# First pairs of the seven-product scheme: fifth and sixth operand first, GpSimd's subtractions last, the fourth a difference of differences

## The chip, the core and the metric

The kernel runs on one core of one Trainium2 chip. A core has a matmul engine (TensorE, PE in the profile; PEld is its loading of weights), VectorE (DVE), ScalarE (ACT), GpSimd (POOL) and SyncE (SP), which issues most of the DMAs here. Each engine works through its own queue in order, and waits on semaphores of the others. PE and the others share the on-chip buffers (SBUF) and the matmul banks (PSUM). The metric is the device time of one execution in microseconds; lower is better.

## What is computed

A decoder trunk of two layers over 1024 positions of width 1024, in float32. Layer 0 mixes tokens with a chunked gating MLP, layer 1 with dilated attention (three groups of dilation 1, 4 and 16); each is followed by a squared-ReLU MLP, and a norm ends it.

```python
def reference(x, mix_norm_g, mlp_norm_g, final_norm_g, a_w_in, ..., w_up, w_down):
    h = x
    for layer in range(DEPTH):
        y = _rms_norm(h, mix_norm_g[layer])
        if layer % N_MIXERS == 0:
            y = _chunk_gating_mixer(y, ...)
        else:
            y = _dilated_attention_mixer(y, ...)
        h = h + y
        y = _rms_norm(h, mlp_norm_g[layer])
        h = h + jnp.square(jax.nn.relu(y @ w_up[layer])) @ w_down[layer]
    return _rms_norm(h, final_norm_g)
```

## The kernel before

**Layout.** Activations are held transposed: `h` is eight tiles of 128 features by 1024 positions. Work goes over two halves of 512 positions (`s` = 0, 1). Every float32 product is made of three passes on rounded operands: a tile is split (`split`, L202) into a high part, copied by ACT (L203), and a low part, subtracted by DVE (L204), and PE runs high·high, high·low, low·high (`three`, L359). So one 128x128 by 128x512 product is three matmuls, and a sum over four feature blocks is twelve.

**Seven products.** The large products (MLP up, MLP down, q/k/v of attention) use a scheme of seven products for a 2x2 block product in place of eight. The two columns are the position halves `s`, the two rows are feature halves `j`. `Terms` (L439) holds the activation operands. With y0, y1 for `s` = 0 and z0, z1 for `s` = 1: operands 1, 2, 3 are y0, y1, z1; t5 = z0 - y0; t6 = z1 - t5; t7 = z1 - z0; t4 = y1 - t6. Each is four tiles (`k` = 0..3), and each tile is split into a `pair` in the pool "s" of 38 slots. `Weights` (L382) loads four raw blocks and forms the seven weight operands, its additions on GpSimd (L401 to L406), its splits on ACT and DVE (tiles "wp", a ring of eight).

**An opening.** Three times the norm of `h` is taken and a stage with seven products starts: MLP 0 (`mlp`, L716), attention (L1474 to L1491) and MLP 1. `first` (L447) scales the eight tiles of `s` = 0 into `kept` and splits them; `second` (L461) does so for `s` = 1 into `raws`, then forms t5 (L476) and t6 (L477) on DVE in the ring "b" of two buffers (`spare`, L131; variables `t1`, `t2`), t7 (L478) and t4 (L479) on GpSimd in place in `kept`, and splits t5 and t6; `rest` (L484) splits t7 and t4. Since z is late, the first pair of weight tiles is done in the classical way (`classical`, L430: eight products, four banks, first all of `s` = 0, then all of `s` = 1); the operands of the seven are made meanwhile. Then PE goes on with products 1, 3, 6, 2, 7, 5, 4 of the next weights.

In an MLP the four banks of a classical half go through Relu (L688) and Square (L689) on ACT, and the result is stored to DRAM (L684) as hidden tiles. Product 1 of the seven is copied out of its bank by ACT at L750 (`first_sum`), and product 2 is then added up in the same bank, so it waits for that copy. In attention the four banks are q, k and v of unit 0 and q of unit 1, evacuated by `out` (L1128): v by ACT (L1079), q and k by ACT (L1121) and DVE (L1122). The next products need banks that these free. Soon after, the first scores, their softmax (DVE L1217, ACT L1219) and the transposes of its result (PE L187) come in.

At the start of attention `h` is stored to DRAM (`hd`, L1489 to L1491) and loaded again later (L1468), which frees eight slots.

**What sets the order.** PE's order is the program's own. `Flow` (L45) keeps a clock of PE's time and runs side tasks (generators such as `second`) when their time has come: a `yield` of so many ns is how long the planner gives a step, and `flow.until` moves the planner's clock on until a condition holds. Only the order comes from this; no engine waits for it. The instructions of the other engines and of the DMA queues are ordered by the framework's scheduler from dependencies, buffers and priority; priority follows the order in the program, and `tc.high_priority(offset=PRIO)` moves instructions ahead. Buffers of a ring are handed out when their last readers are done: "t" has eleven (`temp`), "b" two (`spare`), "r" four (`raw`), PSUM three "mm" and five "at" banks.

Of the kernel before, what the change touches and what calls it, by code (L numbers as in the profile page):

```python
# [10 lines left out]
F32 = mybir.dt.float32  # L11
# [6 lines left out]
P = 128  # L18
D = 1024
S = 1024  # L20
# [92 lines left out]
def trunk(ctx: ExitStack, tc: tile.TileContext, xT, w_u, w_v, w_o, w_s, b_s, w_qkv, w_bo, rel,  # L113
# [17 lines left out]
    def spare():  # L131
        return tpool.tile([P, HALF], F32, tag="b", name="b", bufs=2)
# [22 lines left out]
    def pair(name="y"):  # L155
        return Pair(slot((P, 2, HALF), F32R, name))
# [282 lines left out]
    class Terms:  # L439


        def __init__(self):
            self.blocks = {(j, s): [] for j in range(2) for s in range(2)}
            self.t = {1: self.blocks[0, 0], 2: self.blocks[1, 0], 3: self.blocks[1, 1], 4: [], 5: [], 6: [], 7: []}
            self.kept = []

        def first(self, sq, gi):  # L447

            r = sq.rms()
            yield LAT["rms"]  # L450
            pb = spread(r)
            for k in range(KT):
                if k < 4:
                    self.kept.append(slot((P, 2, HALF), F32, "keep"))
                y = self.kept[k % 4][:, k // 4, :]
                nc.vector.scalar_tensor_tensor(y, h[k][:, sq.cols], vec[:, gi, k:k + 1], pb, op0=ALU.mult, op1=ALU.mult)
                x = pair().split(y)
                yield LAT["tile"]
                self.blocks[k // 4, 0].append(x)

        def second(self, sq, gi):  # L461
            r = sq.rms()
            yield 2 * LAT["rms"]
            pb = spread(r)
            raws = [slot((P, 2, HALF), F32, "raws") for _ in range(4)]
            for j in range(2):
                for k in range(4):
                    o, y = 4 * j + k, raws[k][:, j, :]
                    nc.vector.scalar_tensor_tensor(y, h[o][:, sq.cols], vec[:, gi, o:o + 1], pb, op0=ALU.mult, op1=ALU.mult)
                    x = pair().split(y)  # L470
                    yield LAT["tile"]
                    self.blocks[j, 1].append(x)
            tt = nc.vector.tensor_tensor
            for k, two in enumerate(raws):
                (z0, z1), (y0, y1), t1, t2 = *([t[:, j, :] for j in range(2)] for t in (two, self.kept[k])), spare(), spare()
                tt(t1, z0, y0, op=ALU.subtract)  # L476
                tt(t2, z1, t1, op=ALU.subtract)  # L477
                nc.gpsimd.tensor_tensor(y0, z1, z0, op=ALU.subtract)  # L478
                nc.gpsimd.tensor_tensor(y1, y1, t2, op=ALU.subtract)  # L479
                yield 2 * LAT["tile"]  # L480
                self.t[5].append(pair("t1").split(t1))
                self.t[6].append(pair("t2").split(t2))

        def rest(self):  # L484

            for k, x in enumerate(self.kept):
                t3, t4 = x[:, 0, :], x[:, 1, :]
                if k == 3:
                    t4 = temp()
                    nc.gpsimd.tensor_copy(t4, x[:, 1, :])  # L490
                self.t[7].append(pair("t3").split(t3))
                self.t[4].append(pair("t4").split(t4))

    def start_terms(sq, s, gi, terms):
        flow.add((terms.second if s else terms.first)(sq, gi), (1 + s) * LAT["sum"])


    vg = {}
# [187 lines left out]
    def squared(t, src=None):  # L686

        nc.scalar.activation(t, t if src is None else src, AF.Relu)  # L688
        nc.scalar.activation(t, t, AF.Square)  # L689
# [26 lines left out]
    def mlp(layer, x, first, last):  # L716
# [8 lines left out]
        for s in range(2):  # L725
            banks = [at_bank() if (n < 2) == (s == 1) else mm_bank() for n in range(4)]
            if s == 0:
                banks = [mm_bank() if n < 3 else at_bank() for n in range(4)]
            classical(x, first, s, banks)
            for b, (q, i) in zip(banks, tiles):  # L730
                c[q, i, s] = temp()
                with tc.high_priority(offset=PRIO):
                    squared(c[q, i, s], b)
                what = {(0, 0): 1, (1, 0): 2, (0, 1): (0, 1), (1, 1): 3}[i, s]
                kept(q, {what: c[q, i, s]})
            if s == 0:
                w = up_weights(2)
                for _ in w.steps():
                    pass
# [255 lines left out]
    xa = Terms()  # L995
    firsts = []

    def begin_attention(sq):
        if not firsts:
            firsts.extend(plain(qkv(*t)) for t in (((0, 0), (0, 1)), ((0, 2), (1, 0))))  # L1000
            start_terms(sq, 0, 2, xa)
        else:
            start_terms(sq, 1, 2, xa)

    mlp(0, terms, first, [(half(s), begin_attention) for s in range(2)])

# [468 lines left out]
    for s in range(2):  # L1475
# [3 lines left out]
        classical(xa, firsts, s, banks)  # L1479
        if s == 1:  # L1480
            U[0].bias = bias_tile(U[0].hp, U[0].g)
        for b, tile in zip(banks, ((0, 0), (0, 1), (0, 2), (1, 0))):
            out(tile, s, b)
        if s == 0:
            w = Weights(qkv(*quads[0]), late=FIRST)
            for _ in w.steps():
                pass
    xa.rest()
    hd = [dram.tile([P, S], F32, tag=f"hd{k}", name=f"hd{k}", bufs=1) for k in range(KT)]  # L1489
    for k in range(KT):  # L1490
        nc.sync.dma_start(hd[k], h[k])  # L1491

    for n, two in enumerate(quads):
        wn = Weights(qkv(*quads[n + 1])) if n + 1 < len(quads) else None
# [123 lines left out]
```

## Time and profile before

| | us |
| --- | --- |
| median of 3 runs | 2185.85 |
| lowest to highest | 2181.33 to 2186.66 |
| profiled execution, its time | 2182.13 |
| span of the profile, first to last instruction | 2180.4 |
| PE busy | 2121.8 (97%) |
| DVE busy | 1647.1 (76%) |
| ACT busy | 1126.3 (52%) |
| GpSimd busy | 600.9 (28%) |

A row of the timeline has the start and the length in us, the engine, the line of the code, the operation, the tiles written and read (buffer numbers left out), the shape, and the count of instructions merged in it. In brackets stands the engine's idle time before it, and which instruction's end released it. In a row of the waits stand the waiting engine and line, then the engine, tile and line waited for, the total, the number and the longest. A row for one line of the code has the least, median and greatest duration in ns, and the first and last start in us. A row of the stretches has the stretch, its length, then for PE, PEld, DVE, ACT and POOL the busy time with the number of instructions, the granted PE clock, and DMA. A matmul's end is modelled, so the time of a run of matmuls is taken from start to start. "y" are split tiles of `kept` and `raws`; "t" as a matmul's operand is a split t4, t5, t6 or t7.

### The profile page before, as it was taken

The numbers are of one execution on the slowest core, as the hardware profiler recorded it, in microseconds if no ns is written. First come the engines' busy times: TensorE is split into PE (matmuls) and PEld (weight loads), VectorE is DVE, ScalarE is ACT, GpSimd is POOL, SyncE is SP. The second block draws the span as 40 slices with busy tenths as digits, with TensorE's granted clock in tenths as the row PEclk, the third lists the DMA queues.
The fourth block names the chain that finished last, engine by engine and source line by source line (L and its number), as shares of the span: only waits on it lengthen the run. The fifth ranks groups of instructions, "written<-read, shape, count | busy, mean of one in ns | idle before, by whom it ended". The sixth has DMA issues, their size and how long they took to land.

```text
span 2180.4 us, 30158 instructions
## 1 busy us (share of the span) xinstructions
PE 2121.8 (97%) x10242; PEld 1755.2 (80%) x10242; DVE 1647.1 (76%) x2987; ACT 1126.3 (52%) x2266; POOL 600.9 (28%) x442
## 2 busy tenths in 40 slices
PE   7999999999999999998999999999999999999998
PEld 5888887888878888886888788887878888788887
DVE  5875349676689888878787877878786666988886
ACT  5743225555564444346665656665455555544443
POOL 1100115333223322533212222201343232333345
PEclk9999999999999999999999999999999999999999
DMA  6221213456354444321211111141055543644432
GB/s 222 87 88 45 62 41 96 158 189 198 138 176 160 159 141 137 105 82 39 52 46 46 43 48 45 46 147 62 20 169 193 184 159 113 203 150 146 157 104 78
DMA packets 158814, 247.04 MB, mean 113 GB/s; under 512 B 33481, under 2 KB 47940, under 8 KB 158660
## 3 DMA queue, kind: packets, MB, share of 16 engines
q1 hardware_dynamic: 157760, 243.89, 34.3%
q8 instruction: 80, 1.31, 0.2%
q10 hardware_dynamic: 900, 1.23, 0.2%
q14 instruction: 74, 0.61, 0.1%
HBM read 180.41 MB, written 64.66 MB: 112 GB/s over the span
## 4 chain that ended last, share of the span: by engine, by line
PE 82%; DVE 9%; ACT 3%; issue 2%; DMA 2%; POOL 0%; SPq 0%; DVEq 0%; ACTq 0%; POOLq 0%
PE at L180 41%; PE mm L180 39%; PE at L187 2%; DVE wp L204 2%; DVE t L204 1%; ACT t L1219 1%; ACT wp L203 1%; DVE k L1122 1%; DMA t<-hid 1%; DVE tr L204 0%; DMA r<-in_w_v 0%; DVE h L332 0%; DVE q L1122 0%; DVE h L893 0%; DMA h<-hd 0%
## 5 line engine op out<-in xcount | busy, mean ns | idle before, releaser
L203 ACT ACTIVATE wp<-r 128x512 fp32r<-128x512 f32 (+3 forms) x492 | 295.1, 605 | 458.0 <-PE at L180 287.7
L180 PE MATMUL mm<-y,wp 128*128 128x512 f32 x1608 | 405.2, 398 | 12.8 <-ACT t L750 6.6
L180 PE MATMUL at<-hx,wp 128*128 128x512 f32 x1770 | 413.8, 390 | 3.8 <-DVE wp L204 2.2
L204 DVE TENSOR_TENSOR wp<-r,wp 128x512 fp32r<-128x512 f32 (+3 forms) x492 | 380.9, 778 | 40.1 <-ACT wp L203 36.3
L180 PEld LDWEIGHTS at<-hx,wp 128*128 128x128 f32 x1770 | 331.8, 188 | 75.1 <-DVE h L893 3.3
L180 PEld LDWEIGHTS mm<-y,wp 128*128 128x128 f32 x1608 | 303.2, 191 | 80.4 <-ACT t L750 7.5
L180 PE MATMUL at<-t,wp 128*128 128x512 f32 x1344 | 314.3, 389 | 0.0
L180 PEld LDWEIGHTS at<-t,wp 128*128 128x128 f32 x1344 | 252.7, 188 | 52.7 <-DVE t L756 0.2
L401 POOL TENSOR_TENSOR t<-r 128x512 f32<-128x512 f32 (+3 forms) x78 | 112.8, 1446 | 624.8 <-DMA r<-in_w_dn 270.3
L403 POOL TENSOR_TENSOR r<-r 128x512 f32<-128x512 f32 (+3 forms) x78 | 118.4, 1518 | 326.9 <-DVE wp L204 320.1
L180 PE MATMUL mm<-t,wp 128*128 128x512 f32 x768 | 192.6, 398 | 0.0
L204 DVE TENSOR_TENSOR hx<-t,hx 128x512 fp32r<-128x512 f32 x192 | 179.8, 948 | 5.7 <-ACT hx L203 5.6
L261 POOL TENSOR_TENSOR t<-t 128x512 f32<-128x512 f32 (+1 forms) x54 | 69.1, 1280 | 387.3 <-ACT t L252 385.4
L180 PE MATMUL mm<-hx,wp 128*128 128x512 f32 x708 | 171.8, 389 | 0.0
L180 PEld LDWEIGHTS mm<-t,wp 128*128 128x128 f32 x768 | 141.2, 189 | 29.8
L180 PE MATMUL mm<-y,whi 128*128 128x512 f32 x512 | 158.1, 390 | 0.0
L180 PEld LDWEIGHTS mm<-hx,wp 128*128 128x128 f32 x708 | 132.8, 188 | 28.1 <-DVE b L919 0.6
L893 DVE TENSOR_TENSOR h<-h,at 128x512 f32<-128x512 f32 x144 | 97.5, 679 | 55.4 <-PE at L180 55.3
L180 PE MATMUL at<-y,wp 128*128 128x512 f32 x552 | 138.1, 391 | 0.0
L756 DVE TENSOR_TENSOR t<-t,at 128x512 f32<-128x512 f32 x116 | 79.0, 683 | 74.9 <-PE at L180 74.7
L203 ACT ACTIVATE hx<-t 128x512 fp32r<-128x512 f32 x192 | 118.4, 628 | 27.8 <-DMA t<-hid 23.4
L406 POOL TENSOR_TENSOR r<-r 128x512 f32<-128x512 f32 (+3 forms) x78 | 107.2, 1374 | 79.8 <-issue 54.0
(213 smaller groups left out, 3244.0 us busy)
## 6 DMA issues: line engine op xcount, KB each, us to landing
t<-hid SPq DMA_DIRECT2D x194, 256.0 KB, 5.0
hid<-t SPq DMA_DIRECT2D x140, 256.0 KB, 2.7
r<-in_w_up SPq DMA_DIRECT2D x128, 256.0 KB, 2.8
r<-in_w_dn SPq DMA_DIRECT2D x88, 256.0 KB, 2.7
r<-in_w_qkv SPq DMA_DIRECT2D x72, 256.0 KB, 2.6
hid<-b SPq DMA_DIRECT2D x56, 256.0 KB, 2.7
r<-in_w_v SPq DMA_DIRECT2D x48, 256.0 KB, 3.0
h<-in_xT SPq DMA_DIRECT2D x16, 256.0 KB, 4.5
```

Of the source, the lines that this page charges most:

```text
L180: nc.tensor.matmul(out, lhsT, rhs, **kw)
L187: nc.tensor.transpose(out, src, ident)
L203: nc.scalar.activation(hi, src, AF.Copy)
L204: nc.vector.tensor_tensor(lo, src, hi.bitcast(F32), op=ALU.subtract)
L261: nc.gpsimd.tensor_tensor(self.acc, self.acc, sq, op=ALU.add)
L401: tt(r3, r[0, 0], r[1, 0], op=ALU.subtract)
L403: tt(r[1, 1], r[1, 0], r[0, 0], op=ALU.subtract)
L406: tt(r[0, 0], r[0, 1], r[1, 1], op=ALU.subtract)
L756: nc.vector.tensor_tensor(out, x, y, op=ALU.add)
L893: engine.tensor_tensor(hs[i, s], hs[i, s], src, op=ALU.add)
L1122: nc.vector.scalar_tensor_tensor(lo, a, sc, hi.bitcast(F32), op0=ALU.mult, op1=ALU.subtract)
L1219: nc.scalar.activation(p[:, c], p[:, c], AF.Exp, bias=m, scale=-1.0, accum_out=dn)
```

## The change

In `Terms`: `first` also subtracts, on GpSimd and in place, y0 from y1 once y1 is split; t5 and t6 are formed in tiles of the general ring "t" of eleven, for each `k` one step ahead of their splits, and the planner is given 1600 ns a step; after all of them GpSimd forms t7 = z1 - z0 and t4 = (y1 - y0) - t7, and sets `formed`, for which `rest` waits in the planner. A callable `then` runs once the rows of `s` = 1 are scaled: in attention it stores `h` to DRAM, which stood after `xa.rest()`. In `mlp` only the Relus out of the banks keep the high priority; the four Squares and the stores follow them. In attention the classical outputs of `s` = 1 are evacuated in the order 2, 3, 0, 1. PE's instructions are the same in number; GpSimd has four more subtractions an opening.

```diff
-            self.kept = []
+            self.kept, self.formed = [], False
...
                 self.blocks[k // 4, 0].append(x)
-
-        def second(self, sq, gi):
+                if k >= 4:
+                    nc.gpsimd.tensor_tensor(y, y, self.kept[k % 4][:, 0, :], op=ALU.subtract)
+
+        def second(self, sq, gi, then=None):
...
-            tt = nc.vector.tensor_tensor
-            for k, two in enumerate(raws):
-                (z0, z1), (y0, y1), t1, t2 = *([t[:, j, :] for j in range(2)] for t in (two, self.kept[k])), spare(), spare()
-                tt(t1, z0, y0, op=ALU.subtract)
-                tt(t2, z1, t1, op=ALU.subtract)
-                nc.gpsimd.tensor_tensor(y0, z1, z0, op=ALU.subtract)
-                nc.gpsimd.tensor_tensor(y1, y1, t2, op=ALU.subtract)
-                yield 2 * LAT["tile"]
-                self.t[5].append(pair("t1").split(t1))
-                self.t[6].append(pair("t2").split(t2))
+            if then:
+                then()
+            tt, sums = nc.vector.tensor_tensor, []
+            for k in range(5):
+                if k < 4:
+                    z, y0, t1, t2 = raws[k], self.kept[k][:, 0, :], temp(), temp()
+                    tt(t1, z[:, 0, :], y0, op=ALU.subtract)
+                    tt(t2, z[:, 1, :], t1, op=ALU.subtract)
+                    sums.append((t1, t2))
+                if k:
+                    for p, t in zip((5, 6), sums[k - 1]):
+                        self.t[p].append(pair(f"t{p}").split(t))
+                yield LAT["tile"]
+            for z, y in zip(raws, self.kept):
+                nc.gpsimd.tensor_tensor(y[:, 0, :], z[:, 1, :], z[:, 0, :], op=ALU.subtract)
+                nc.gpsimd.tensor_tensor(y[:, 1, :], y[:, 1, :], y[:, 0, :], op=ALU.subtract)
+            self.formed = True

         def rest(self):

+            flow.until(lambda: self.formed)
...
                 with tc.high_priority(offset=PRIO):
-                    squared(c[q, i, s], b)
+                    nc.scalar.activation(c[q, i, s], b, AF.Relu)
+            for q, i in tiles:
+                nc.scalar.activation(c[q, i, s], c[q, i, s], AF.Square)
...
+    hd = [dram.tile([P, S], F32, tag=f"hd{k}", name=f"hd{k}", bufs=1) for k in range(KT)]
+
+    def spill():
+        for k in range(KT):
+            nc.sync.dma_start(hd[k], h[k])
...
-            start_terms(sq, 1, 2, xa)
+            start_terms(sq, 1, 2, xa, spill)
...
-        for b, tile in zip(banks, ((0, 0), (0, 1), (0, 2), (1, 0))):
+        outs_ = list(zip(banks, ((0, 0), (0, 1), (0, 2), (1, 0))))
+        for b, tile in outs_[2:] + outs_[:2] if s else outs_:
             out(tile, s, b)
...
     xa.rest()
-    hd = [dram.tile([P, S], F32, tag=f"hd{k}", name=f"hd{k}", bufs=1) for k in range(KT)]
-    for k in range(KT):
-        nc.sync.dma_start(hd[k], h[k])
```

More of the change, by code (lines that the diff above doesn't have):

```diff
@@ L492, in rest, with start_terms @@
                 self.t[4].append(pair("t4").split(t4))
-    def start_terms(sq, s, gi, terms):
-        flow.add((terms.second if s else terms.first)(sq, gi), (1 + s) * LAT["sum"])
+    def start_terms(sq, s, gi, terms, *then):
+        flow.add((terms.second if s else terms.first)(sq, gi, *then), (1 + s) * LAT["sum"])
     vg = {}
```

## The prediction

> **What bounds the kernel now.** I read the page first, then PE's waits, then PE's rows where those waits lie, and last the queues of ACT, DVE and GpSimd at the same moments. From the page:
>
> ```profile
> PE 2121.8 (97%) x10242; PEld 1755.2 (80%) x10242; DVE 1647.1 (76%) x2987; ACT 1126.3 (52%) x2266; POOL 600.9 (28%) x442
> ```
>
> PE is the bound, so an edit is worth what it takes out of PE's idle time and its slowed matmuls. Two of PE's longest waits name tiles beside the change (us, times, longest); in the stretch with the second, PE is busy 4.35 us of 10 at a granted clock of 0.77:
>
> ```profile
> PE mm L180 <- ACT t L750: 6.6, 2, 4.3
> PE mm L180 <- ACT t L1079: 5.6, 1, 5.6
> ```
>
> ```profile
> 990.00:1000.00 10.00, 4.35 (x14) 3.24 (x13) 9.90 (x11) 7.84 (x13) 5.16 (x4) 0.77 0.10 25
> ```
>
> They are the three openings, where a stage turns from classical products to the seven: MLP 0 near 367, attention near 992, MLP 1 near 1589. Each is sized from PE's rows, first MLP 0:
>
> ```profile
> 365.67 1.29 PE L180 MATMUL at<-t,wp 128*128 128x512 f32 x5
> 369.31 4.22 PE L180 MATMUL mm<-y,wp 128*128 128x512 f32 x12 [2.35 <-ACT t L750]
> 373.34 11.59 PE L180 MATMUL at<-t,wp 128*128 128x512 f32 x48
> 384.76 2.88 PE L180 MATMUL mm<-y,wp 128*128 128x512 f32 x12
> 387.48 5.60 PE L180 MATMUL at<-t,wp 128*128 128x512 f32 x24
> ```
>
> Undisturbed, 12 matmuls take 2.72 us from start to start (384.76 to 387.48), 0.227 each. The five of the first row are over at 366.80; the 60 up to 384.76 should take 13.60 and take 17.96. The opening loses **4.36**: the gap, and 2.0 of slow matmuls behind it. MLP 1, then attention:
>
> ```profile
> 1585.81 2.88 PE L180 MATMUL at<-t,wp 128*128 128x512 f32 x12
> ...
> 1592.97 4.51 PE L180 MATMUL mm<-y,wp 128*128 128x512 f32 x12 [4.28 <-ACT t L750]
> 1597.32 7.87 PE L180 MATMUL at<-t,wp 128*128 128x512 f32 x34
> ```
>
> ```profile
> 987.47 4.24 PE L180 MATMUL mm<-y,wp 128*128 128x512 f32 x18
> 997.35 4.21 PE L180 MATMUL mm<-y,wp 128*128 128x512 f32 x9 [5.65 <-ACT t L1079]
> 1001.49 1.32 PE L180 MATMUL at<-k,q 64*128 64x128 f32 x12
> ...
> 1009.63 0.33 PE L187 MATMUL at<-ident,t 128*128 128x128 f32 x1 [1.30 <-ACT t L1219]
> ```
>
> MLP 1: the 12 matmuls from 1585.81 end at 1588.53. The next 12 should end 2.72 later; they end 8.79 later, at 1597.32, so **6.07** is lost. Attention: the 18 matmuls (six classical ones and the first of the seven products) end at 991.55; the next start at 997.35, and nine take 4.14 where 2.04 would do: 5.80 + 2.10 = **7.90** lost by 1001.49. A second wait, of the transposes for the first softmax, follows at 1009.63.
>
> ACT works in order, and what PE wants from it (L750, L1079) stands behind splits that come late. MLP 0, then attention:
>
> ```profile
> 358.63 0.63 ACT L203 ACTIVATE t<-b 128x512 fp32r<-128x512 f32 x1 [2.02 <-DVE b L477]
> 359.17 3.22 ACT L203 ACTIVATE t<-keep 128x512 fp32r<-128x512 f32 x6
> ...
> 368.65 0.61 ACT L750 ACTIVATE t<-mm 128x512 f32<-128x512 f32 x1
> ```
>
> ```profile
> 991.98 0.63 ACT L203 ACTIVATE t<-b 128x512 fp32r<-128x512 f32 x1 [3.37 <-DVE b L476]
> ...
> 996.25 1.05 ACT L1079 ACTIVATE t<-mm 128x512 f32<-128x512 f32 x1
> ```
>
> The "b" ring has two buffers. The next pair of t1, t2 waits until GpSimd has read t2 (L479) and both splits are done; and while GpSimd runs, a subtraction on DVE takes about 1.7 instead of 0.69 (two in 3.48, one in 0.69):
>
> ```profile
> 342.58 0.69 DVE L477 TENSOR_TENSOR b<-raws,b 128x512 f32<-128x512 f32 x1
> 343.19 3.48 DVE L204 TENSOR_TENSOR t<-b,t 128x512 fp32r<-128x512 f32 x2
> ...
> 365.93 0.67 DVE L204 TENSOR_TENSOR wp<-r,wp 128x512 fp32r<-128x512 f32 x1
> ```
>
> ```profile
> L478 POOL TENSOR_TENSOR keep<-raws x12: 1292/1710/1846, 331.3 to 1579.2; 128x512 f32<-128x512 f32 x12
> ```
>
> **Fifth and sixth first, in general buffers.** The number and size of DVE's and ACT's instructions stay as they are. What goes is the ring's turn-round: GpSimd no longer stands between one k and the next. In MLP 0 the last "b" split ran at 358.63, and 9.48 us of ACT's work (the "keep" splits, weight splits, four Relus, four Squares) lay between 359.17 and L750. At 342.58 the second k had its t2, and GpSimd had two of its eight subtractions behind it. With all t1, t2 at hand it needs for the other six and the two weight steps L403 and L406 eight times 1.74 (half of 3.48, the pace at which DVE and GpSimd take turns), 13.9: until 356.5, an estimate from these rows. PE's classical products end three products of 12 before 366.80, at 358.64, so the "keep" splits are through by then. ACT owes PE four Relus and L750, five times 0.54 (3.22 / 6), 2.7, and has until 366.80. The gap goes, and the slow matmuls with it. Next late is weight 2: its low part, done at 366.60 (365.93 + 0.67), is wanted by the product's third matmul at 367.25, so it holds even if DVE gains nothing. 4.36 at best, 0 if ACT's order stays; I take **4.2**, since the wait of 2.02 at 358.63 is what filled that queue.
>
> In MLP 1 the same split is the bound that is left:
>
> ```profile
> 1589.13 0.68 DVE L204 TENSOR_TENSOR wp<-r,wp 128x512 fp32r<-128x512 f32 x1
> ```
>
> It ends at 1589.81 and is wanted at 1588.53 + 0.45 = 1588.98: between 0 and 0.83 late, as DVE does or doesn't gain. Of 6.07 I take **5.7**.
>
> **Attention.** Here DVE is the tight engine:
>
> ```profile
> 957.25 0.75 DVE L469 SCALAR_TENSOR_TENSOR raws<-h,vec,at 128x512 f32<-128x512 f32 x1 [3.48 <-PE at L187]
> ...
> 971.60 0.71 DVE L477 TENSOR_TENSOR b<-raws,b 128x512 f32<-128x512 f32 x1
> 975.40 0.69 DVE L1070 TENSOR_TENSOR V<-at,V 128x512 fp32r<-128x512 f32 x1 [3.09 <-ACT V L1069]
> ...
> 1002.13 4.69 DVE L204 TENSOR_TENSOR t<-keep,t 128x512 fp32r<-128x512 f32 x6
> ...
> 1008.77 0.27 DVE L1217 CUSTOM_DVE_ANT_0 t<-at,b 128x128 f32<-128x128 f32 x1
> ```
>
> The 5.65 at L1079 goes, as ACT's splits no longer wait; evacuating the mm banks first brings L1079 ahead of two other tiles. But then PE comes 7.9 earlier to the transposes of 1009.63, which need the softmax of 1008.77, and DVE has nearly all of its work still to do. So this term is what DVE gains before 1008.77: at least the 3.09 that it stood idle at 975.40, which the freed subtractions fill; at most PE's 7.9, if L1217 also passes the six "keep" splits of 1002.13 (4.69). How DVE's queue will be ordered this trace can't show; the present one puts the splits first, so I stay near the low end: **4.5**. Below 3.09 it comes only if GpSimd's turns fill that idle time.
>
> **GpSimd.** The fourth operand as a difference of differences costs four more subtractions an opening, in the first half's pass: 4 x 1.71 = 6.8 of GpSimd, and on DVE up to 4 x 1.05 (1.74 less 0.69). In attention they end in the 3.48 that DVE idles ahead of 957.25, waiting for PE's turn: 0, and at worst 4.2 - 3.48 = 0.7 for what that cover doesn't hold. Eight subtractions stay in the second half, now without a claim on t2; nothing on PE waits for them before products 7 and 4, the fifth and last of the seven in this first pair.
>
> **Buffers and the planner.** Eight sums go through the ring "t" of eleven, which also takes the evacuated banks. No row shows a wait for it; the nearest is the 2.02 at the "b" ring, so 0 to 2 an opening. I take 0: a sum is free after its split, without GpSimd. The new wait for "formed" is the planner's, not an engine's: five steps of 1600 in place of four of 3200 let it pass earlier than before, so PE's order stays. 0.
>
> **Relu apart from Square, order of evacuation.** Four Squares (2.2 at 0.54) lose their priority and can go behind L750; the stores of hidden tiles on SP's queue wait for them, and the next weights' loads behind those. The 48 matmuls from 373.34 carry no wait, so these loads come in time now; I take 0, bounds minus 2.2 to plus 2.2. In attention the mm banks are emptied first, so L1079 passes two tiles of the at banks; that is part of the 7.9.
>
> **h to DRAM.** The stores run early already:
>
> ```profile
> 932.36 12.58 SPq L1491 DMA_DIRECT2D hd<-h  x8
> ```
>
> They are issued by 944.94, before the second half's rows are scaled (from 957.25), so moving the statement up brings them no earlier: 0. Should the queue put them behind the scaling (over by 971.60), they would hold SP until 984.2, still ahead of the end of classical at 988.83: 0 again.
>
> Sum: 4.2 + 5.7 + 4.5 = 14.4. The profiled execution took 2182.13 (span 2180.4), so 2167.7; the median of 2185.85 lies 3.7 above it, and in its terms the forecast is **2171.4**.
>
> The trace has the 2.35 gap followed by 12 matmuls in 4.03 (369.31 to 373.34), not 2.72. The Trainium skill (TensorE: Matmul & The Clock Gate, "What's actually happening") has the clock halved only after an idle window of about 3.4 us; by that, the gap in MLP 0 would cost its 2.35 alone and the sum would be 2.35 + 5.7 + 4.5 = 12.6, not 14.4. The row decides: a gap below that length did slow the matmuls here.
>
> **Rivals** (times in the median's terms).
> - *DVE is the bound in attention all along.* The stall only moves from 997 to the transposes, which start at 1009.6 as before. For it: DVE's 9.90 of 10 busy in 990 to 1000. Against: the 3.09 idle. Gain 4.2 + 5.7 = 9.9: 2176.0.
> - *The change doesn't unblock ACT.* The splits' order on ACT stays ahead of L750 and L1079. Then only the Squares (2.2) leave the queue in each MLP, and about 1 (one evacuation, L1079's 1.05) comes from the other order in attention: gain 5.4, 2180.5. For it: the order is the scheduler's, not the code's. Against: the ring's waits are in the rows.
> - *GpSimd's tail holds ACT (slower).* If its eight subtractions start only after the last t2, the "keep" splits on ACT wait for them, with L1079 behind. In attention the seven sums left at 971.60 end, by 1.74 each, at 983.8; eight subtractions and the weights' two reach 1001.2; with a copy (1.71 at most), two splits (1.1) and L1079 (1.05) it is 1005.1, and PE resumes 7.8 later than at 997.35. With the MLPs as before that is 2193.6; if each still gains the Squares' 2.2, 2189.3. It turns slower from where the last subtraction ends after about 993.5 (997.35 less those 3.9). Against: GpSimd's first subtraction ran at 331.3, 11 us before the second k's t2, so its queue isn't kept for last.
>
> **Chances.** The forecast has 0.62, the first rival 0.15, the second 0.13, the third 0.10. The forecast's own gain runs from 9 to 20: below, the Squares' 2.2 and a ring wait against it; above, all of 4.36 + 6.07 + 7.90 and the 1.30 at 1009.63, 19.6. That is 2166 to 2177; with the scatter of the runs shown (2181.33 to 2186.66, half of it 2.7) below and the second rival above, the range is 2163 to 2181. A measurement of this kernel can tell about 0.3%, 6.6 us, from no change. Faster by more: the forecast and the first rival, 0.77. Within it: the second and half of the third, 0.18. Slower: the other half, 0.05.
>
> **What would show it.** Right: no PE wait on L750 in either MLP and the 12 matmuls behind it in 2.72; L1079 before 991.6; the "t" splits no longer waiting on DVE's "b"; a PE wait for L1219 as the largest left in attention. Wrong: "keep" splits on ACT waiting for GpSimd; PE waiting for weight 2 or the seventh operand; loads of the next weights late behind the hidden stores.

## The result, and the profile after

| | before | after |
| --- | --- | --- |
| median, us (17 runs each) | 2185.10 | 2187.91 |
| lowest to highest | 2180.01 to 2188.96 | 2185.54 to 2192.01 |
| span of the profiled execution | 2180.4 | 2184.8 |

The ratio is 1.0015, 95% interval 1.0008 to 1.0021. By the bound of 0.3% this is no change, with a sign: a little slower. The forecast was 2171.4, range 2163 to 2181.

The page of the kernel after has the engines' busy times, and its waits of PE have the lines that replace those of before (L750 is now L762, L1079 is L1097, L756 is L768, L476 and L477 are L481 and L482, L478 and L479 are L489 and L490):

```profile
PE 2120.8 (97%) x10242; PEld 1752.7 (80%) x10242; DVE 1660.3 (76%) x2987; ACT 1126.3 (52%) x2266; POOL 617.3 (28%) x454
```

```profile
PE mm L180 <- ACT t L1097: 9.1, 1, 9.1
...
PE mm L180 <- ACT t L762: 6.0, 2, 5.2
...
PE mm L180 <- DVE h L332: 2.5, 4, 1.3
...
PE at L180 <- DVE t L768: 2.2, 1, 2.2
```

DVE does the same 2987 instructions in 13.2 us more; GpSimd, with twelve more, is busy 16.4 us longer. The two waits that were to go are there: the one in attention has grown from 5.6 to 9.1, that in MLP 0 from 2.4 to 5.2; only MLP 1's shrank, to 0.8. PE's timeline after, in MLP 0, attention and MLP 1:

```profile
364.12 2.88 PE L180 MATMUL at<-t,wp 128*128 128x512 f32 x12
372.18 4.95 PE L180 MATMUL mm<-y,wp 128*128 128x512 f32 x12 [5.18 <-ACT t L762]
376.96 9.28 PE L180 MATMUL at<-t,wp 128*128 128x512 f32 x40
...
991.32 4.24 PE L180 MATMUL mm<-y,wp 128*128 128x512 f32 x18
1004.68 3.77 PE L180 MATMUL mm<-y,wp 128*128 128x512 f32 x9 [9.12 <-ACT t L1097]
1008.38 0.95 PE L180 MATMUL at<-k,q 64*128 64x128 f32 x12
...
1594.89 3.06 PE L180 MATMUL mm<-y,wp 128*128 128x512 f32 x12 [0.84 <-ACT t L762]
1597.78 5.60 PE L180 MATMUL at<-t,wp 128*128 128x512 f32 x24
1605.54 5.76 PE L180 MATMUL at<-t,wp 128*128 128x512 f32 x24 [2.16 <-DVE t L768]
```

By the prediction's count (0.227 a matmul, start to start), attention has lost 13.36 - 4.08 = 9.28 at the gap and 3.70 - 2.04 = 1.66 in the nine slow matmuls: 10.94, where it was 7.90.

For a sum over everything I took, for each matmul in the trace, the distance to the next one's start less the median distance for its shape and line, and added this up for the 100 us around each opening. "PE's loss" below is this number.

| PE's loss, us | MLP 0 (300 to 400) | attention (950 to 1050) | MLP 1 (1550 to 1650) | all else |
| --- | --- | --- | --- | --- |
| before | 5.0 | 17.6 | 5.9 | 55.2 |
| after | 9.7 | 20.2 | 4.0 | 54.3 |

The four differences (+4.7, +2.6, -1.9, -0.9) make 4.5; the span grew by 4.4. So, in these two profiles, the whole result is made in the three openings. (The medians lie 2.8 apart. Some 1.6 us of such a difference in one opening can be the phase of the clock; see the last section.)

What is late there is seen on DVE. The views of one line of code give the least, median and greatest duration of the sums t5 and t6; before:

```profile
L476 DVE TENSOR_TENSOR b<-raws,keep x12: 673/686/1780, 325.4 to 1577.4; 128x512 f32<-128x512 f32 x12
...
L477 DVE TENSOR_TENSOR b<-raws,b x12: 675/692/1820, 335.8 to 1581.6; 128x512 f32<-128x512 f32 x12
```

After:

```profile
L481 DVE TENSOR_TENSOR t<-raws,keep x12: 670/1776/1784, 340.5 to 1577.2; 128x512 f32<-128x512 f32 x12
...
L482 DVE TENSOR_TENSOR t<-raws,t x12: 677/1668/1779, 341.2 to 1578.4; 128x512 f32<-128x512 f32 x12
```

The median sum went from 0.69 to 1.7 us, at the same number and size. GpSimd's timeline in attention shows what runs beside them: in after its eight subtractions stand in one unbroken row, at the same time as DVE's sums.

```profile
976.20 1.80 POOL L489 TENSOR_TENSOR keep<-raws 128x512 f32<-128x512 f32 x1 [12.78 <-DVE t L481]
978.08 1.63 POOL L490 TENSOR_TENSOR keep<-keep 128x512 f32<-128x512 f32 x1
...
988.30 1.62 POOL L490 TENSOR_TENSOR keep<-keep 128x512 f32<-128x512 f32 x1
991.15 1.67 POOL L403 TENSOR_TENSOR r<-r 128x512 f32<-128x512 f32 x1 [1.23 <-DVE wp L204]
992.90 1.62 POOL L406 TENSOR_TENSOR r<-r 128x512 f32<-128x512 f32 x1
```

In before the ring of two parted these subtractions, and the weight sums L403 and L406 ran between them, from 978.02 to 981.34:

```profile
978.02 1.62 POOL L403 TENSOR_TENSOR r<-r 128x512 f32<-128x512 f32 x1 [4.29 <-issue]
979.72 1.62 POOL L406 TENSOR_TENSOR r<-r 128x512 f32<-128x512 f32 x1
```

In after they end at 994.52. ACT, in order, waits for them, with the evacuation behind:

```profile
994.55 1.15 ACT L203 ACTIVATE wp<-r 128x512 fp32r<-128x512 f32 x2 [10.17 <-POOL r L406]
...
996.65 3.73 ACT L203 ACTIVATE t<-keep 128x512 fp32r<-128x512 f32 x7
...
1000.81 1.04 ACT L1139 ACTIVATE q<-at 128x512 fp32r<-128x512 f32 x1
...
1002.70 1.04 ACT L1139 ACTIVATE k<-at 128x512 fp32r<-128x512 f32 x1
1003.54 1.09 ACT L1097 ACTIVATE t<-mm 128x512 f32<-128x512 f32 x1
```

### The profile page after: what moved, and what is told of

It is laid out like the page before. It is cut to its first block, busy times and chain, and to the rows that moved or that the text cites. A ratio compares the mean times of both kernels' runs of the same rounds, so it can differ in the third digit from the quotient of the medians.

```text
span 2184.8 us, 30158 instructions
## 1 busy us (share of the span) xinstructions
PE 2120.8 (97%) x10242; PEld 1752.7 (80%) x10242; DVE 1660.3 (76%) x2987; ACT 1126.3 (52%) x2266; POOL 617.3 (28%) x454
## 3 DMA queue, kind: packets, MB, share of 16 engines
q10 hardware_dynamic: 900, 1.23, 0.2%
## 4 chain that ended last, share of the span: by engine, by line
PE 81%; DVE 10%; ACT 3%; DMA 3%; issue 2%; SPq 1%; POOL 0%; DVEq 0%; ACTq 0%; POOLq 0%
PE at L180 40%; PE mm L180 39%; PE at L187 2%; DVE wp L204 2%; DVE t L204 1%; DMA t<-hid 1%; DVE t L481 1%; DVE t L482 1%; DVE y L204 1%; SPq L169 1%; ACT wp L203 1%; DVE k L1140 1%; ACT t L1237 0%; DMA r<-in_w_up 0%; DVE q L1140 0%
## 5 line engine op out<-in xcount | busy, mean ns | idle before, releaser
L204 DVE TENSOR_TENSOR wp<-r,wp 128x512 fp32r<-128x512 f32 (+3 forms) x492 | 388.3, 793 | 39.5 <-ACT wp L203 36.0
L403 POOL TENSOR_TENSOR r<-r 128x512 f32<-128x512 f32 (+3 forms) x78 | 116.4, 1493 | 318.9 <-DVE wp L204 316.9
L768 DVE TENSOR_TENSOR t<-t,at 128x512 f32<-128x512 f32 x116 | 79.0, 683 | 76.2 <-PE at L180 76.0
L406 POOL TENSOR_TENSOR r<-r 128x512 f32<-128x512 f32 (+3 forms) x78 | 106.8, 1370 | 82.5 <-issue 53.8
```

The costliest lines, as they stand in the source:

```text
L204: nc.vector.tensor_tensor(lo, src, hi.bitcast(F32), op=ALU.subtract)
L403: tt(r[1, 1], r[1, 0], r[0, 0], op=ALU.subtract)
L406: tt(r[0, 0], r[0, 1], r[1, 1], op=ALU.subtract)
L768: nc.vector.tensor_tensor(out, x, y, op=ALU.add)
```

## The experiments

**Theory 1, the burst:** without the ring GpSimd runs its eight subtractions in one row beside DVE's sums and splits; the two engines slow each other, and weight sums, weight splits and the evacuations behind them on ACT come late. **Theory 2, ACT's order:** the evacuation order and the Squares, or the sums' stay in the ring "t", are what hold L762 and L1097. Ratios are to the kernel before on the same chip.

**x1_tail_dve:** the kernel after, the second half's eight subtractions on DVE.

```diff
-                nc.gpsimd.tensor_tensor(y[:, 0, :], z[:, 1, :], z[:, 0, :], op=ALU.subtract)
-                nc.gpsimd.tensor_tensor(y[:, 1, :], y[:, 1, :], y[:, 0, :], op=ALU.subtract)
+                nc.vector.tensor_tensor(y[:, 0, :], z[:, 1, :], z[:, 0, :], op=ALU.subtract)
+                nc.vector.tensor_tensor(y[:, 1, :], y[:, 1, :], y[:, 0, :], op=ALU.subtract)
```

> The changed kernel with the eight subtractions of the second half (t7, t4) on DVE in place of GpSimd. Theory 1 (burst): freed from the ring, GpSimd runs its eight subtractions in one row beside DVE's eight sums, each sum takes 1.7 instead of 0.69, and behind them come the weights' low splits, GpSimd's L403 and L406 and so ACT's queue. Then here the sums take 0.7, the wait for L1097 falls from 9.1 to under 4, that for L762 in MLP 0 from 5.2 to under 2.4, and the time is some 8 us under the changed kernel, about 2180. Theory 2 (order and buffers: ACT's order, the late Squares or the ring t): DVE has 8 x 0.69 = 5.5 us more to do an opening and nothing is freed, so the waits stay or grow: 2188 to 2193.

2170.98 us, ratio 0.9943 (0.9929 to 0.9956). Giving DVE eight more instructions an opening saves some 16 us against after (1.0015 less 0.9943, of 2185). One of these subtractions takes 0.68 on DVE, and the sums are back at 0.68:

```profile
L482 DVE TENSOR_TENSOR t<-raws,t x12: 678/684/693, 340.8 to 1559.3; 128x512 f32<-128x512 f32 x12
...
L489 DVE TENSOR_TENSOR keep<-raws x12: 677/682/686, 354.7 to 1570.5; 128x512 f32<-128x512 f32 x12
```

PE's wait on L762 is gone, L1097's is 5.1, and MLP 1 loses 0.0. Theory 1 holds, though its sizes were off: the gain is twice what it expected, and the wait on L1097 was to fall under 4.

**x2_first_dve:** the kernel after, the first half's four subtractions (L461) on DVE.

```diff
-                    nc.gpsimd.tensor_tensor(y, y, self.kept[k % 4][:, 0, :], op=ALU.subtract)
+                    nc.vector.tensor_tensor(y, y, self.kept[k % 4][:, 0, :], op=ALU.subtract)
```

> The changed kernel with the four new subtractions of the first half (y1 - y0) on DVE in place of GpSimd. Theory 1: the new wait of 1.34 for h (L332) in MLP 0 goes, as no split of y is slowed in front of that addition; the waits for L762 and L1097 stay. 1 to 3 us under the changed kernel: 2185 to 2187. Theory 2: nothing of this counts, 2188; DVE's own 4 x 0.69 could make it 1 to 2 slower.

2191.73 us, ratio 1.0039 (1.0024 to 1.0054): a miss. In MLP 0's first half DVE is itself what PE waits for, the additions to `h` (L332); four more instructions ahead of them made that wait longer, not shorter. PE's timeline of x2:

```profile
313.08 0.94 PE L180 MATMUL mm<-y,wp 128*128 128x512 f32 x3 [2.93 <-DVE h L332]
...
314.63 3.73 PE L180 MATMUL mm<-y,wp 128*128 128x512 f32 x9
```

In after the same wait was 1.34. The waits of the second half (L762 5.2, L1097 9.1) were the same as in after.

**x3_evac_only:** the kernel before, with Relu and Square apart and the order of output, and nothing else.

```diff
-                    squared(c[q, i, s], b)
+                    nc.scalar.activation(c[q, i, s], b, AF.Relu)
+            for q, i in tiles:
+                nc.scalar.activation(c[q, i, s], c[q, i, s], AF.Square)
...
-        for b, tile in zip(banks, ((0, 0), (0, 1), (0, 2), (1, 0))):
+        outs_ = list(zip(banks, ((0, 0), (0, 1), (0, 2), (1, 0))))
+        for b, tile in outs_[2:] + outs_[:2] if s else outs_:
```

> The kernel before with only the Relus apart from the Squares and the other order of evacuation; operands as before. Theory 1: these edits are harmless, 0 to 3 us under the kernel before (2182 to 2185): L750 comes up to 2.2 earlier, L1079 about 1. Theory 2: they are what costs, so the waits are as long as in the changed kernel and the time is 2187 to 2189.

2181.13 us, ratio 0.9987 (0.9976 to 0.9997). Harmless, perhaps a small gain. Of PE's waits, that on the first sum's copy, here L752, falls from 6.6 to 4.3 and a wait for DVE comes instead; attention's is untouched.

```profile
PE mm L180 <- ACT t L1081: 5.6, 1, 5.6
PE mm L180 <- ACT t L752: 4.3, 2, 3.0
...
PE at L180 <- DVE t L758: 1.9, 1, 1.9
```

**x4_no_tail:** the kernel after without the eight subtractions; products 7 and 4 run on other data, so its time is that of less work.

```diff
-                nc.gpsimd.tensor_tensor(y[:, 0, :], z[:, 1, :], z[:, 0, :], op=ALU.subtract)
-                nc.gpsimd.tensor_tensor(y[:, 1, :], y[:, 1, :], y[:, 0, :], op=ALU.subtract)
+                pass
```

> The changed kernel without the eight subtractions of the second half: t7 and t4 are taken from what stands in their buffers, so the products 7 and 4 work on other data, in the same shapes. Theory 1: no contention is left in the second half and the whole of the waits for L762 and L1097 goes: 10 to 16 us under the changed kernel, 2172 to 2178. Theory 2: ACT's order and the ring stay, so at most 3 us under it, 2185.

2168.41 us, ratio 0.9932 (0.9918 to 0.9946), below the range of theory 1. L762's wait is gone, L1097's is 1.4. So GpSimd's eight subtractions cost some 18 us (1.0015 less 0.9932), and doing them on DVE, about 2 of that (x1; the two intervals overlap). Theory 2 falls with x1, x3 and x4: the order edits cost nothing, and with them in place the time comes down.

The next two separate the ring from the engine.

**y1_before_dve:** the kernel before, its L478 and L479 on DVE; the ring of two stays.

```diff
-                nc.gpsimd.tensor_tensor(y0, z1, z0, op=ALU.subtract)
-                nc.gpsimd.tensor_tensor(y1, y1, t2, op=ALU.subtract)
+                nc.vector.tensor_tensor(y0, z1, z0, op=ALU.subtract)
+                nc.vector.tensor_tensor(y1, y1, t2, op=ALU.subtract)
```

> The kernel before, with its eight second-half subtractions an opening (L478, L479) on DVE instead of GpSimd; the ring of two for t1, t2 stays. Burst theory: what costs is GpSimd subtracting beside DVE, in before too, so without it the sums on DVE take about 0.69 each and the time is 2171 to 2176, close to the run with the tail on DVE (2171.0), ring or no ring. Ring theory (the prediction's reading: the turn-round of the ring is what held ACT): GpSimd is out of the turn, but both splits of a k still stand between it and the next, so only part of the gain comes: 2177 to 2182.

2173.91 us, ratio 0.9959 (0.9946 to 0.9971), as the burst theory had it.

**y3_ring_only:** the kernel before, t5 and t6 in the ring of eleven.

```diff
-                (z0, z1), (y0, y1), t1, t2 = *([t[:, j, :] for j in range(2)] for t in (two, self.kept[k])), spare(), spare()
+                (z0, z1), (y0, y1), t1, t2 = *([t[:, j, :] for j in range(2)] for t in (two, self.kept[k])), temp(), temp()
```

> The kernel before with t1 and t2 in the general ring of eleven in place of the ring of two, and nothing else: GpSimd's two subtractions still stand behind each k's sums in the program. Burst theory: with the ring gone GpSimd and DVE meet as in the kernel after, whatever the statements' order: 2182 to 2188, the waits on L1079 and L750 not less than in before. Rival (the ring is what held ACT, and the kernel after loses by putting GpSimd's subtractions last and adding four): 2172 to 2178, with the wait on L1079 under 3.

2186.49 us, ratio 1.0011 (1.0003 to 1.0020). One word makes what the whole change made; its waits of PE in attention and the MLPs are

```profile
PE mm L180 <- ACT t L1079: 9.1, 1, 9.1
PE mm L180 <- ACT t L750: 7.7, 2, 5.1
```

and its t5 sums took 1.78 in the median:

```profile
L476 DVE TENSOR_TENSOR t<-raws,keep x12: 670/1779/1785, 338.8 to 1576.1; 128x512 f32<-128x512 f32 x12
```

| ratio to before | subtractions on GpSimd | on DVE |
| --- | --- | --- |
| ring of two | 1 (before) | 0.9959 (y1) |
| ring of eleven | 1.0011 (y3), 1.0015 (after) | 0.9943 (x1) |

The ring moves the time by 0.11 to 0.16%, some 3 us, up with the subtractions on GpSimd and perhaps down with them on DVE (there the two intervals overlap); the engine moves it by 0.4 to 0.7%, 9 to 16 us. (x1 has the change's other edits too.)

Nor did the ring of two keep the engines apart. Take DVE's 128x512 TENSOR_TENSOR instructions of the second halves (325 to 400, 935 to 1010, 1530 to 1610) and add up what each took above 0.69: 44.8 us in before, 49.0 in y3, 47.6 in after, but 21.5 in y1 and 18.3 in x1. With or without the ring DVE loses about the same to GpSimd; without it more of the loss falls on the sums, which the splits wait for.

Two runs ask how the burst costs.

**z3_wsum_dve:** the kernel after with L403 and L406 of each opening's first weights on DVE, so that they don't stand behind the burst.

```diff
             r, tt = self.r, nc.gpsimd.tensor_tensor
+            t2 = nc.vector.tensor_tensor if self.late == FIRST else tt
...
-            tt(r[1, 1], r[1, 0], r[0, 0], op=ALU.subtract)
+            t2(r[1, 1], r[1, 0], r[0, 0], op=ALU.subtract)
...
-            tt(r[0, 0], r[0, 1], r[1, 1], op=ALU.subtract)
+            t2(r[0, 0], r[0, 1], r[1, 1], op=ALU.subtract)
```

> The kernel after, GpSimd's burst as it is, with the two last weight sums (L403, L406) of the first seven-product weights of each opening on DVE, so that no weight stands behind the eight subtractions on GpSimd's queue. If the burst costs by its length on GpSimd (weights late, and ACT's splits of them holding L762 and L1097): most of the gain of the runs without the burst comes, 2172 to 2178, and L1097's wait falls under 5. If it costs by slowing DVE's sums and splits from 0.69 to 1.7: DVE has two more such subtractions, 2184 to 2190, the waits as in after.

2183.40 us, ratio 0.9996 (0.9984 to 1.0007): under the second range and far above the first, some 4 us below after. The queue behind the burst is a part of the cost. The larger part stays, and ACT's wait in attention only became shorter (10.17 to 6.19); it now ends with DVE:

```profile
993.57 1.15 ACT L203 ACTIVATE wp<-r 128x512 fp32r<-128x512 f32 x2 [6.19 <-DVE r L407]
```

**z4_held:** the kernel after with GpSimd's eight held until the last t6 is formed.

```diff
+            for y in self.kept:
+                nc.gpsimd.tensor_copy(y[:, 0, 0:1], sums[3][1][:, 0:1])
             for z, y in zip(raws, self.kept):
```

> The kernel after with GpSimd's eight subtractions held until the last t6 is formed: four copies of one column of it (128x1) are put ahead of them, into columns that they overwrite, so the result is the same. The weights' two sums then come before the burst, and DVE's eight sums run without GpSimd beside them. Burst theory by DVE's slowed sums: the sums take about 0.69 again, the t splits come early, 2176 to 2183. Rival 3 of the prediction (GpSimd's tail itself holds ACT's splits of keep, with L1097 behind): the wait on L1097 stays at 9 or more, 2187 to 2193.

2189.19 us, ratio 1.0021 (1.0011 to 1.0031). The sums took 0.68 again, as expected, and yet nothing was gained: the burst now ran beside the splits, and L406 ended at 998.05.

```profile
L481 DVE TENSOR_TENSOR t<-raws,keep x12: 669/684/1776, 342.8 to 1576.8; 128x512 f32<-128x512 f32 x12
```

```profile
998.08 1.15 ACT L203 ACTIVATE wp<-r 128x512 fp32r<-128x512 f32 x2 [12.50 <-POOL r L406]
```

So it isn't the sums as such. In both places tried, the burst lengthens DVE's and GpSimd's work together, and ACT waits for the last of it. Of my own theory the narrow form (only the slowed sums) fell here. What stands is that both queues count; no run separates their shares further, since in attention the hold also put L403 and L406 behind most of the burst.

The rest looks for the best place of these operands on DVE.

**y2_all_dve:** t4 = y1 - t6 on DVE right behind t6, t7 at the tail on DVE, nothing in the first half.

```diff
-                if k >= 4:
-                    nc.gpsimd.tensor_tensor(y, y, self.kept[k % 4][:, 0, :], op=ALU.subtract)
...
                     tt(t2, z[:, 1, :], t1, op=ALU.subtract)
+                    tt(self.kept[k][:, 1, :], self.kept[k][:, 1, :], t2, op=ALU.subtract)
...
-                nc.gpsimd.tensor_tensor(y[:, 0, :], z[:, 1, :], z[:, 0, :], op=ALU.subtract)
-                nc.gpsimd.tensor_tensor(y[:, 1, :], y[:, 1, :], y[:, 0, :], op=ALU.subtract)
+                nc.vector.tensor_tensor(y[:, 0, :], z[:, 1, :], z[:, 0, :], op=ALU.subtract)
```

> The kernel after with no subtraction of the openings on GpSimd: none in the first half, t4 = y1 - t6 on DVE right behind t6, and t7 = z1 - z0 on DVE at the tail. Against the run with only the tail on DVE (2171.0) it saves the 1.34 wait on h in MLP 0 (and what the first half loses in the others) and does four additions fewer an opening, all on DVE: eight instead of twelve. Burst theory: 2165 to 2170. If the first half's subtractions on GpSimd are free: 2170 to 2172. If DVE's own load is now the bound, t4 ahead of the splits of t5 and t6 costs as much as it saves: 2171 to 2174.

2174.88 us, ratio 0.9956 (0.9944 to 0.9968): the third case, just above its range. MLP 0 loses 4.9, by a wait of 2.3 on DVE's L766 and slow matmuls behind it.

**z1_tail_two:** the same with t4 = y1 - t6 at the tail.

```diff
-                    tt(self.kept[k][:, 1, :], self.kept[k][:, 1, :], t2, op=ALU.subtract)
...
-            for z, y in zip(raws, self.kept):
+            for z, y, (_, t2) in zip(raws, self.kept, sums):
                 nc.vector.tensor_tensor(y[:, 0, :], z[:, 1, :], z[:, 0, :], op=ALU.subtract)
+                nc.vector.tensor_tensor(y[:, 1, :], y[:, 1, :], t2, op=ALU.subtract)
```

> The kernel after with t4 = y1 - t6 and t7 = z1 - z0, both on DVE and both behind the splits of t5 and t6; nothing on GpSimd in the first half. It is the run with the tail on DVE (2171.0) without the first half's four GpSimd subtractions, and the run y2 (2174.9) with t4 behind the splits instead of ahead of them. If y2 lost by t4 standing ahead of the splits (its MLP 0 waited 2.3 for DVE t L766): 2167 to 2171, that wait near 1. If keeping t6 in the ring of eleven until the tail holds evacuations: a new wait of PE on a tile of ring t, 2172 to 2176.

2172.43 us, ratio 0.9942 (0.9929 to 0.9954). MLP 0 loses 2.0, the wait on the sum behind product 2 is not among the longest, and no wait for the ring came. Its time falls into the second range without the wait named there, and can't be told from those of x1 and y2.

**y4_banks_first** and **z2_tail_two_banks:** y2 and z1 with PE's classical order for the second half in attention changed, so that the mm banks are complete first.

```diff
-    def classical(x, first, s, banks):
+    def classical(x, first, s, banks, order=(0, 1, 2, 3)):
...
-            for t, b in enumerate(banks):
+            for t in order:
+                b = banks[t]
...
-        classical(xa, firsts, s, banks)
+        classical(xa, firsts, s, banks, (2, 3, 0, 1) if s else (0, 1, 2, 3))
```

> The run without any GpSimd subtraction (y2), with PE's classical order for the second half in attention changed from banks 0, 1, 2, 3 to 2, 3, 0, 1, so that the two mm banks which the seven products need are complete first; the copy L1097 then has no reason to come behind two others. Burst theory: the wait on L1097 was the queue ahead of it on ACT, which is already short in y2; 0 to 3 us less than y2. Order theory (ACT's order of evacuation is what costs in attention, and the edit of the output order didn't change it): 3 to 5 us less than y2, and the wait on L1097 gone.

> The same with PE's classical order for the second half in attention 2, 3, 0, 1 (mm banks complete first). In y4 this took L1097's wait from 5.5 to 3.1 and the time by 2.3. Burst theory: again 1 to 3 less than without it, 2165 to 2170. If the tail's subtractions on DVE set the end in attention anyway: no difference, within 1 us.

2172.56 us, ratio 0.9948 (0.9934 to 0.9961), and 2169.15 us, ratio 0.9926 (0.9913 to 0.9938): 2.3 and 3.3 less than without it, though in each pair the intervals overlap. The wait in attention fell from 5.5 to 3.1 and from 4.3 to 2.9. ACT's timeline of z2 has the copy out of the mm bank now ahead of the at banks:

```profile
989.70 1.05 ACT L1096 ACTIVATE t<-mm 128x512 f32<-128x512 f32 x1
990.54 1.12 ACT L1138 ACTIVATE q<-at 128x512 fp32r<-128x512 f32 x1
```

**v1_no_pool:** z2 with the edit of z3, beside **v2_z2_again**, z2 on the same chip.

> The run with the tail of two on DVE and the mm banks first (2169.15), with the two last weight sums (L403, L406) of each opening's first seven-product weights on DVE too. There, ACT's splits of these weights in attention still waited 4.4 for GpSimd's L406, and PE 2.9 for the copy L1096 behind them. If that queue is what is left of the attention's loss: the wait falls under 1 and the time to 2165 to 2167. If DVE, with four more sums in the three openings' most crowded stretches, is now what holds them: 2168 to 2172, the wait unchanged or moved to DVE's weight splits.

> The run with the tail of two on DVE and the mm banks first once more, on the same chip as the run with the weight sums on DVE, so that the two can be compared: 2167 to 2171 as before.

2167.16 us, ratio 0.9920 (0.9907 to 0.9934), and 2170.66 us, ratio 0.9937 (0.9925 to 0.9950). v1's median lies between the two ranges. The wait on the evacuation is gone altogether. But attention loses 16.2, as with it (15.2 in v2): the stall moved to the transposes behind the first softmax. PE's waits of v1:

```profile
PE at L187 <- ACT t L1237: 5.0, 7, 1.7
```

v1 has the lowest median of all that do the whole work; from z2 the intervals don't part it.

## Why the prediction was wrong

**The step that failed** is the first of "Fifth and sixth first": "The number and size of DVE's and ACT's instructions stay as they are. What goes is the ring's turn-round". Number and size stayed; the duration of the sums didn't, with a median of 0.69 before and 1.7 after. The prediction priced GpSimd's work at the pace of taking turns (1.74) and put nothing on DVE's eight sums for the same turns, though the row it quoted for that pace was DVE's own (3.48 for two), and though it did charge DVE 1.05 for each of the four subtractions of the first half. The ring's wait was read as what made ACT's splits late, and taking it away didn't make them early: with the ring alone gone (y3) the ratio is 1.0011 instead of 14 us less, while taking the eight subtractions off GpSimd gains with the ring (y1, 0.9959) as without it (x1, 0.9943).

**MLP 0, 4.2 forecast.** The ring's waits did go. But the last sum, L482, came at 361.19, and ACT's timeline has its split later than the 358.63 of before, behind a longer wait:

```profile
362.32 0.63 ACT L203 ACTIVATE t<-t 128x512 fp32r<-128x512 f32 x1 [3.89 <-DVE t L482]
362.86 3.74 ACT L203 ACTIVATE t<-keep 128x512 fp32r<-128x512 f32 x7
...
371.53 0.59 ACT L762 ACTIVATE t<-mm 128x512 f32<-128x512 f32 x1
```

GpSimd was to be through at 356.5; its last subtraction ended at 360.72: its first began at 341.22, ten microseconds after that of before, and it then waited twice for DVE's late sums (1.23 and 0.63). The opening lost 4.7 more, not 4.2 less; 1.6 of this is the first half's, below. (Of the 4.36 that the prediction sized, the 2.0 of slow matmuls hung on the clock's phase as well; see the last section.) In x1 there is no gap at L762, so the reading of ACT's queue was right: free the splits and L762 is in time.

**MLP 1, 5.7 forecast.** 1.9 came. The gap at L762 went from 4.28 to 0.84, but DVE's additions behind product 2 (L768) came late, the wait of 2.16, which no rival had. Without the burst (x1, y2, z1, z2) MLP 1 loses nothing, so weight 2's low part, the bound named there, holds up nobody once DVE is free.

**Attention, 4.5 forecast.** 2.6 was lost. "Below 3.09 it comes only if GpSimd's turns fill that idle time" named the case and gave it no price. The step "evacuating the mm banks first brings L1079 ahead of two other tiles" failed as well: in after L1097 comes behind q and k of the at banks, and in x3, as in before, behind q. Of the edits tried, only the one to the order in which PE completes the banks (y4, z2) moved the copy ahead.

**GpSimd's first half, priced at 0.** The prediction looked for cover in attention, where it held, and not in MLP 0. There two L461 lie beside a split on DVE of 1.60, ahead of the L332 that PE wanted (DVE's and GpSimd's timelines of after):

```profile
309.75 1.60 DVE L204 TENSOR_TENSOR y<-keep,y 128x512 fp32r<-128x512 f32 x1 [0.70 <-ACT y L203]
311.27 0.68 DVE L332 TENSOR_TENSOR h<-h,mm 128x512 f32<-128x512 f32 x1
```

```profile
310.76 3.41 POOL L461 TENSOR_TENSOR keep<-keep 128x512 f32<-128x512 f32 x2
```

The stretch 300 to 350 loses 2.1 in after, 0.5 in before and in z1, which has no L461: 1.6.

**Buffers, priced at 0.** In MLP 0 the ring "t" did hold up the sums. The first t5 started 0.8 us after the first scaled tile of `s` = 1 in before, and 15.8 us after it both in the kernel after and in y3, so the ring does it:

```profile
325.41 0.69 DVE L476 TENSOR_TENSOR b<-raws,keep 128x512 f32<-128x512 f32 x1
```

```profile
334.49 3.33 SPq L694 DMA_DIRECT2D hid<-t  x4
```

```profile
340.48 0.67 DVE L481 TENSOR_TENSOR t<-raws,keep 128x512 f32<-128x512 f32 x1
```

The first row is before's, the others after's. By the semaphores of the trace, the sum at 340.48 waits for the last of four stores of hidden tiles, which landed at 340.19; these tiles come from the same ring. So all of GpSimd's eight subtractions fell after 341, where in before two were over by 338. With the subtractions on DVE the late start costs little (x1 loses 1.5 from 350 to 400).

**Right.** Relu apart from Square: x3, with the order of output too, gains 2.8 us (0.7 to 5.2); the bounds were 2.2 either way. The stores of `h` are issued from 936.2 to 948.5, before 932.4 to 944.6, still ahead of the scaling: 0.

**The rivals.** The third (GpSimd's tail holds ACT, 2189.3 to 2193.6, chance 0.10) came nearest: ACT does wait for L406 and L1097 does stand behind. Its condition, that the eight start only after the last t6, wasn't met in after; it was met in z4, at 2189.19, where the wait on the copy was 10.5. By its ratio, 1.0021, z4 is 2190.4 in the prediction's terms, inside that range. In after the same end is reached by the sums being slowed. The argument against this rival, GpSimd's first subtraction at 331.3, rested on the early first sum that the ring "t" took away. The first rival (the stall moves to the transposes) is what v1 shows, once everything ahead of it is gone. The second was right that ACT's splits stay ahead of L750 and L1079, but the gain of 5.4 that it kept didn't come.

Left open: how much of v1's remaining 16 us in attention is DVE's own load and how much the softmax's chain.

## What to carry to other kernels

When a change sets the work of two engines side by side, price both at the pace that the trace has for them side by side. A wait in a row shows what came last, not what a change of it is worth: take it away alone first (y3) before building on it. A larger ring isn't free either, when the tiles it shares are still on their way to DRAM. A short elementwise step is not free on an idle engine: here it took 1.7 us on GpSimd, slowed its neighbour by 1.0, and would have taken 0.68 on the engine that was thought too busy. The order of the evacuations in the source didn't bring the copy forward here; changing when its input is complete did.

## What the runs showed of the hardware

- DVE and GpSimd slow each other when both work on two operands from SBUF, mostly by taking turns. In after's attention both engines' instructions follow one another every 1.6 to 1.8 us (POOL 976.20, 978.08; DVE's sums 1.67 to 1.78), where a DVE sum takes 0.68 alone (x1) and a GpSimd one 1.27 to 1.29 (the least of L491 and L492 in z4: 1.285, 1.271). The Trainium skill (SBUF — State Buffer, "SBUF: two separate sides") has this as an exclusive lock on a shared port pair, held for a whole instruction, which a DVE instruction with two SBUF inputs takes against a GpSimd one that reads SBUF; the trace agrees that they alternate, but 0.68 and 1.27 make 1.95, and the pace is 1.7. DVE's scaling (scalar_tensor_tensor, L456 and L471) with an operand in PSUM took 0.74 in the median both alone (37 of them in x2) and beside GpSimd (9).
- The turns aren't always even: in y1 GpSimd's copy (L490) ran beside seven DVE splits and took 6.16 us, not the 0.94 of the same line in MLP 0; ACT waited for it, and PE 7.4 behind ACT. That gap is 7.4 of the 19.2 that y1 loses in attention.
- PE's matmuls behind a gap are slow (0.43 a matmul in place of 0.227) while the granted clock is 0.50, and the length of the gap alone doesn't decide whether this comes. z2 and v2 are the same kernel, with the same gap in attention; in z2 (first row) nine matmuls took 3.85 from start to start, in v2 2.27:

```profile
990.80 3.92 PE L180 MATMUL mm<-y,wp 128*128 128x512 f32 x9 [2.88 <-ACT t L1096]
```

```profile
993.80 2.33 PE L180 MATMUL mm<-y,wp 128*128 128x512 f32 x9 [2.87 <-ACT t L1096]
```

The clock's records say why. Inside each execution the stretches at 0.50 last 3.41 us or a multiple of it (but for the last, which the end cuts off), and they all start on one grid of 3.41, whose phase differs from execution to execution. In before's MLP 0 the gap of 2.35 left PE busy for 1.51 of the window 367.42 to 370.83, idle for 1.90, and the next window ran at 0.50:

```profile
367.42:370.83 3.41, 1.51 (x7) 1.25 (x8) 1.40 (x2) 3.40 (x7) 1.47 (x2) 1.00 0.80 212
370.83:374.24 3.41, 3.41 (x10) 2.63 (x9) 3.41 (x4) 1.26 (x2) 2.71 (x2) 0.50 1.05 346
```

In the 16 traces, from 290 us on, every such window in which PE idled for 1.9 or more was followed by one at 0.50; with less it went either way (1.59 in z1 was, 1.86 in x2 wasn't). z2's gap lay in one window; v2's lay across two, with 1.77 as the larger share. The Trainium skill (TensorE: Matmul & The Clock Gate, "What's actually happening") has a free-running window of about 3.4 us, and the clock halved after an idle one; the trace agrees on the window, but it need not be idle throughout.
